# Two weight chunks of each layer by seven block products instead of eight, with sums of weight blocks made in DRAM

## The chip, the cores and the metric

One NeuronCore of one Trainium2 chip runs the kernel. The metric is the device time of one execution in microseconds (us). TensorE (PE) multiplies, VectorE (DVE) and ScalarE (ACT) do the elementwise work, GpSimd (POOL) does a little and issues some DMAs, and SyncE (SP) issues most of them. A loaded weight tile of TensorE ("PEld" in the profile) overlaps its matmuls.

## The reference

Two layers act on x, 256 tokens of 2048 channels. Each layer normalises, multiplies by `w_in` (seven kinds of columns), runs an mLSTM on eight heads and a gated linear recurrence (RG-LRU), gates both and adds their product with `w_out` to x.

```python
u = rms_norm(x, norm_g)
p = u @ w_in
qk, v, o, z_a, ig, fg, xb, z_b = jnp.split(p, SPLIT_AT, axis=-1)
...
h = mlstm_chunkwise(q, k, v, i_pre, log_f)
h = h * jax.nn.sigmoid(o.astype(f32)).reshape(b_, s_, H_A, DV_A)
...
y_a = h.astype(x.dtype) * jax.nn.silu(z_a)
xc = causal_dwconv(xb, lru_conv_w) + lru_conv_b
y_b = rg_lru(xc.astype(f32), w_a, b_a, w_x, b_x, lam).astype(x.dtype) * jax.nn.silu(z_b)
return x + jnp.concatenate([y_a, y_b], axis=-1) @ w_out
```

After both layers a last `rms_norm` gives the output. Everything is float32.

## The kernel before

**Chunks, units and halves.** Of each kind (qk, v, o, z, xb, zb) a layer has four groups g of 512 columns. A chunk, say z of group 2, is 256 tokens times 2048 inputs times 512 columns. Its weights come as four units of 1 MB (128 partitions of 2048 floats) from one DRAM array `ws`, and each unit is worked off in two halves. A half is 128 x 1024 floats, two blocks of 128 inputs by 512 columns.

**Three products for one.** A float32 product is made of three: ACT casts a half to a rounded part wH (L308), DVE subtracts to get the rest wL (L168, in the helper `tt_`), x is split alike into `x_s`, and TensorE multiplies high by high, high by low and low by high (L332). With two blocks of 128 inputs, two blocks of 128 tokens and three products, a half of a plain chunk is 12 matmuls of 128x512. A chunk is 8 halves, 96 matmuls. Its sums for both token blocks stay in two PSUM banks (`new_acc`), from which posts such as `o_post` and `z_post` read.

**Order.** `_sequence` lists the units: for each layer and group the chunks o, qk, v, the products with `w_out` of the group before (`out`), xb, z, the gate product (L761, from `xcs`, the split result of the convolution of xb) and zb. The main loop walks the halves. It splits weights three halves ahead of TensorE (AHEAD), into four buffers each of wH and wL, and loads ahead of that into three buffers of 1 MB (`raw`, L275 and L277, SP's queue). The other work of DVE and ACT (convolutions, softmax-like gates, scans) stands in generators in the list `bg`. After every half `pump` lets them go on for a budget, 1.05 with up to two generators in the list and 2.6 with more. `require` runs them until a named result is there. A scheduler then sets each engine's own order, so that work without a dependency can move far ahead.

**DRAM.** Results change from token to channel order through DRAM: SP writes `moved` (L449), POOL reads it back as `fr` (L450). The residual x stands in DRAM (`x_d`) and POOL adds the products of `out` to it by adding transfers (L901, `accum_op`), half a megabyte each.

**PSUM** has eight banks: two pairs for chunks and four banks for small products, in two tags `aux0` and `aux1` with two buffers each.

Of the kernel before, what the change touches and what calls it, by code (L numbers as in the profile page):

```python
# [63 lines left out]

def _plan():

    return list(dict.fromkeys(item for item, _ in _sequence()))
# [17 lines left out]
def tile_trunk(ctx, tc, x, xt, par, gw, gb, ws, final_g, out):  # L85
# [30 lines left out]
    def new_x_acc():  # L116
        st["xa"] = act.tile([P, 2, D], F32, tag="xacc", name="x_acc")

    def load_x_acc():
        new_x_acc()  # L120
        for c in range(4):
            nc.sync.dma_start(out=st["xa"][:, :, 512 * c : 512 * c + 512], in_=xd[c])

    def store_x(c):
        S.dma_start(out=xd[c], in_=st["xa"][:, :, 512 * c : 512 * c + 512])
# [14 lines left out]

    def load_x(c):
        if c == 0:
            nc.sync.dma_start(out=pars[:, 0, 16:NPAR], in_=par[:, 16:NPAR])
            nc.sync.dma_start(out=pars[:, 1, :], in_=par[:, NPAR : 2 * NPAR])
            nc.sync.dma_start(out=gbs, in_=gb.rearrange("h (l c) -> h l c", l=DEPTH))
            for l in range(DEPTH):
                nc.sync.dma_start(out=gwr[l], in_=gw[l])
            new_ss()
        cs = slice(512 * c, 512 * c + 512)
        nc.sync.dma_start(out=st["xa"][:, :, cs], in_=xv[:, :, cs])  # L150
# [7 lines left out]
    gwr = [small.tile([P, KT, 16], F32, tag="gwr", name=f"gwr{l}") for l in range(DEPTH)]  # L158
# [44 lines left out]
    def tl_lam(nm):  # L203
        return small.tile([P, DEPTH, 16], F32, tag=f"lam_{nm}", name=f"lam_{nm}", bufs=1)

    def lam_gen():
        ql = log1p_exp_half(lam, tl_lam, st["split_end"])
# [11 lines left out]
    bg = deque()  # L219
    timed = []  # L220

    def pump(budget):
        st["credit"] = min(st["credit"] + budget, budget)
        i = 0
        while i < len(bg) and st["credit"] > 0:
            try:
                c = next(bg[i])
            except StopIteration:
                del bg[i]
                continue  # L230
            if c is None:
                break
            if c == "wait":
                i += 1
            else:
                st["credit"] -= c

# [21 lines left out]
    def load_unit(hf):  # L259
        n = st["nload"]  # L260
        st["nload"] += 1
        item, j = hf["at"]
        raw = hf["box"]["raw"] = wraw.tile([P, 2048], F32, tag="raw", name="raw")
        if n < 4:
            w = 512 if n == 0 else 1024
            u = blocks[item, j]
            for o in range(0, 2048, w):
                if o % 1024 == 0:
                    load_xt(n, o // 1024)
                nc.sync.dma_start(out=raw[:, o : o + w], in_=ws[u][:, o : o + w])  # L270
        elif hf["paired"]:
# [14 lines left out]
    def prepare(hf):  # L286
# [16 lines left out]
        opening = n < 4  # L303
# [74 lines left out]
    def rms_stats(l):  # L378
# [6 lines left out]
        st["rstd", l] = rstd  # L385

# [22 lines left out]
    def square_sum(c):  # L409
        for t in range(2):  # L410
            junk = work.tile([P, 512], F32, tag="sF", name="junk")
            S.activation(out=junk, in_=st["xa"][:, t, 512 * c : 512 * c + 512], func=AF.Square,
                         accum_out=st["ss"][:, t, c : c + 1])
# [148 lines left out]
    def e_gen(l, g):  # L562
        while ("nG", l) not in st:
            yield "wait"
        nb = small.tile([P, 2, T], F32, tag="nb", name="nb", bufs=1)
# [26 lines left out]
    def o_post(l, g, acc):  # L592
# [4 lines left out]
        rstd = st["rstd", l]  # L597
# [18 lines left out]
    def qk_post(l, g, acc):  # L616
# [3 lines left out]
        def gen():  # L620
# [18 lines left out]
            while ("E", l, g) not in st or ("v", l, g) not in st:  # L639
                yield "wait"  # L640
            E, em, so, (vH, vL) = st["E", l, g], st["em", l], st["so", l, g], st["v", l, g]
            Pt = work.tile([P, 2, 384], F32, tag="Pt", name="Pt")
# [243 lines left out]
    def out_chunk(l, g, c):  # L886
# [9 lines left out]
        def postfn():  # L896
# [9 lines left out]
            x_acc = st["xa"]  # L906
# [6 lines left out]
            xs = x_acc[:, :, cs]  # L913
            if c == 3:
                tt_(xs, xs, ps, ALU.add)
            for t in range(2):
                xt_ = x_acc[:, t, cs].rearrange("p (c m j) -> p c m j", c=4, m=4)
# [22 lines left out]

    def layer_start(l):
# [7 lines left out]
    def emit_in(l, kind, g):  # L949
        def first_gen(acc):  # L950
            gates(l)
# [12 lines left out]
            yield from gates_tr(l)  # L964

# [8 lines left out]
    def last_out(l, g):  # L974
# [11 lines left out]
        def acc(c, t):  # L986
            if (c, t) not in accs:
# [3 lines left out]
                else:  # L991
                    accs[c, t] = aux("acc_x")
# [16 lines left out]
        def add(c, t, ps, at=0):  # L1009
            xs = st["xa"][:, t, 512 * c + at : 512 * c + at + ps.shape[-1]]  # L1010
# [23 lines left out]
        def finish(t):  # L1034
# [5 lines left out]
            for c in (2, 0, 3, 1):  # L1040
                cs = slice(512 * c, 512 * c + 512)
                xs = st["xa"][:, t, cs]
# [50 lines left out]
    for item in dict.fromkeys(i for i, _ in seq):  # L1093
        kind, l, g = item[0], item[1], item[-1]
        halves = []
# [10 lines left out]
    order_ = [dict(hf, at=(item, j)) for item, j in seq for hf in units[item][j]]  # L1106

    nprep = 0
    for n, hf in enumerate(order_):
# [14 lines left out]
        pump(1.05 if len(bg) <= 2 else 2.6)  # L1124
# [95 lines left out]
```

## Time and profile before

| | |
|---|---|
| time, median of 3 runs | 1491.46 us (1490.43 to 1492.03) |
| the profiled execution | 1491.23 us |
| its span, first to last instruction | 1489.5 us |
| granted TensorE clock | 0.998 |
| ACT busy, DVE busy | 931.6 us (63%), 1060.1 us (71%) |
| moved by DMA | 345.65 MB, mean 232 GB/s |

The profile is of one execution. A row of a group gives line, engine, operation, output and inputs, shape, count, then busy time and the mean duration of one, then the engine's idle time before these instructions and what ended it. A window row gives the busy time of each engine in a stretch, the granted clock, the busy share of the 16 DMA engines and what they moved.

### The profile page before, as it was taken

How to read it: one execution, taken by the hardware profiler on the slowest of the kernel's cores; microseconds unless marked ns; L12 is line 12 of the kernel's file. 1: busy time of each engine (PE TensorE's matmuls, PEld its weight loads, DVE VectorE, ACT ScalarE, POOL GpSimd, SP SyncE). 2: the span in 40 equal slices, each digit the busy share in tenths (PEclk: the TensorE clock that was granted, in tenths of full speed). 3: DMA queues.
4: the chain of work that ended last, by engine and by line, in shares of the span. 5: the costliest groups of instructions: out<-in, count | busy, mean ns of one | idle time of the engine just before them, and what ended most of it. 6: DMA issues, size and time to landing. Idle time of an engine off the chain costs nothing.

```text
span 1489.5 us, 18487 instructions
## 1 busy us (share of the span) xinstructions
PE 1479.5 (99%) x6830; PEld 1236.0 (83%) x6830; DVE 1060.1 (71%) x1448; ACT 931.6 (63%) x1199; POOL 83.1 (6%) x154
## 2 busy tenths in 40 slices
PE   9999999999999999999999999999999999999997
PEld 7888888888888888888888888888888888888886
DVE  6788866676568855778867788765855778557785
ACT  7756864575565845658575667645755567555675
POOL 0020100000000000000000101000000000000002
PEclk9999999999999999999999999999999999999999
DMA  9866767866677666886785766578667777578783
GB/s 341 294 221 223 232 211 214 254 225 214 202 238 234 217 225 216 253 264 226 264 280 193 242 215 240 205 206 250 225 223 214 239 225 234 200 227 269 231 283 109
DMA packets 91370, 345.65 MB, mean 232 GB/s; under 512 B 9984, under 2 KB 30480, under 8 KB 69776
## 3 DMA queue, kind: packets, MB, share of 16 engines
q1 hardware_dynamic: 79472, 306.44, 60.5%
q0 software_dynamic: 9344, 33.58, 9.3%
q10 hardware_dynamic: 2464, 4.47, 0.8%
q8 instruction: 53, 0.87, 0.2%
q14 instruction: 37, 0.30, 0.1%
HBM read 307.20 MB, written 37.24 MB: 231 GB/s over the span
## 4 chain that ended last, share of the span: by engine, by line
PE 96%; DVE 2%; DMA 1%; ACT 1%; issue 0%; POOL 0%; SPq 0%; DVEq 0%; ACTq 0%; POOLq 0%
PE acc L332 86%; PE ps_gt L761 3%; PE acc L345 2%; DVE wL L168 1%; DMA fr<-moved 1%; PE acc L1004 1%; PE acc L1003 1%; PE acc L1002 1%; PE ps_g L499 0%; PE acc_x L1004 0%; PE acc_x L1003 0%; PE acc_x L1002 0%; PE ps_S L648 0%; PE ps_n L590 0%; PE ps_n L588 0%
## 5 line engine op out<-in xcount | busy, mean ns | idle before, releaser
L332 PE MATMUL acc<-wH,x_s 128*128 128x512 f32 x3008 | 930.1, 389 | 0.0
L168 DVE TENSOR_TENSOR wL<-raw,wH 128x1024 fp32r<-128x1024 f32 (+1 forms) x532 | 636.9, 1205 | 326.4 <-ACT wH L308 325.7
L308 ACT CAST wH<-raw 128x1024 fp32r<-128x1024 f32 (+1 forms) x532 | 547.5, 1036 | 393.0 <-PE acc L332 364.7
L332 PEld LDWEIGHTS acc<-wH,x_s 128*128 128x128 f32 x3008 | 564.6, 188 | 117.0
L332 PE MATMUL acc<-wL,x_s 128*128 128x512 f32 x1504 | 584.1, 389 | 0.4 <-DVE wL L168 0.4
L332 PEld LDWEIGHTS acc<-wL,x_s 128*128 128x128 f32 x1504 | 282.3, 188 | 59.1 <-DVE wL L168 0.8
L332 PE MATMUL acc<-wH,yaH 128*128 128x512 f32 x224 | 87.6, 391 | 0.0
L332 PE MATMUL acc<-wH,ybL 128*128 128x512 f32 x224 | 87.3, 390 | 0.0
L332 PE MATMUL acc<-wH,ybH 128*128 128x512 f32 x224 | 87.2, 389 | 0.0
L332 PE MATMUL acc<-wL,ybH 128*128 128x512 f32 x224 | 87.2, 389 | 0.0
L332 PE MATMUL acc<-wH,yaL 128*128 128x512 f32 x224 | 87.2, 389 | 0.0
L332 PE MATMUL acc<-wL,yaH 128*128 128x512 f32 x224 | 87.2, 389 | 0.0
L446 DVE STREAM_TRANSPOSE blk<-tok 128x1024 f32<-128x1024 f32 x33 | 40.9, 1238 | 18.5 <-ACT tok L436 18.5
L436 ACT ACTIVATE tok<-acc,rstd 128x512 f32<-128x512 f32 x46 | 29.1, 685 | 32.9 <-PE acc L332 32.9
L332 PEld LDWEIGHTS acc<-wH,ybL 128*128 128x128 f32 x224 | 42.0, 188 | 9.1 <-DVE ybL L168 0.3
L332 PEld LDWEIGHTS acc<-wH,yaL 128*128 128x128 f32 x224 | 42.0, 188 | 8.9
L332 PEld LDWEIGHTS acc<-wH,ybH 128*128 128x128 f32 x224 | 42.0, 188 | 8.5
L332 PEld LDWEIGHTS acc<-wL,ybH 128*128 128x128 f32 x224 | 42.0, 188 | 8.5
L332 PEld LDWEIGHTS acc<-wL,yaH 128*128 128x128 f32 x224 | 42.1, 188 | 8.3
L332 PEld LDWEIGHTS acc<-wH,yaH 128*128 128x128 f32 x224 | 42.1, 188 | 8.3
L171 DVE SCALAR_TENSOR_TENSOR xc<-ch,pars,xc 128x255 f32<-128x255 f32 (+2 forms) x96 | 43.0, 475 | 4.4 <-ACT xc L420 4.4
L450 POOL DMA_DIRECT2D fr<-moved x34 | 18.8, 554 | 479.4 <-DMA moved<-blk 260.3
(208 smaller groups left out, 1282.1 us busy)
## 6 DMA issues: line engine op xcount, KB each, us to landing
raw<-in_ws_dram SPq DMA_DIRECT2D x168, 1024.0 KB, 5.3
raw<-in_ws_dram SPq DMA_DIRECT2D x190, 512.0 KB, 4.9
fr<-moved POOLq DMA_DIRECT2D x34, 512.0 KB, 5.8
moved<-blk SPq DMA_DIRECT2D x132, 128.0 KB, 2.4
x_d<-stage POOLq DMA_DIRECT2D x24, 512.0 KB, 5.4
x_d<-x_acc ACTq DMA_DIRECT2D x8, 512.0 KB, 7.4
x_acc<-x_d SPq DMA_DIRECT2D x8, 512.0 KB, 4.3
xp<-in_xt_dram SPq DMA_DIRECT2D x8, 256.0 KB, 6.9
```

The lines of the kernel that those rows point to most:

```text
L168: return V.tensor_tensor(out=o, in0=a, in1=b, op=op)
L171: return V.scalar_tensor_tensor(out=o, in0=a, scalar=s, in1=b, op0=op0, op1=op1)
L308: st["wH"] = S.copy(out=H[:, o], in_=r[:, o])
L332: st["mm"] = PE.matmul(o, a_[:, kt, P * t : P * t + P], W[:, k], start=b, stop=z)
L345: PE.matmul(ps[:, ct, T * part : 2 * T], W[:, k, P * ct : P * ct + P], moving, start=first and k == 0 and part == 0, stop=last and k == 3 ...
L436: S.activation(out=by_block(tok, t), in_=acc[:, t, :].rearrange("p (c m j) -> p c m j", c=4, m=4), func=AF.Copy, scale=rstd[:, t : t + 1])
L446: V.transpose(out=blk.rearrange("p m n -> p (m n)"), in_=tok.rearrange("p m c t j -> p (m c t j)"))
L450: back.dma_start(out=fr.rearrange("p a c t i -> p a (c t i)"), in_=moved)
L761: PE.matmul(o, W[:, ib, jl], xs[:, ib, a, :], start=j == 0 and i == 0 and W is Hv and a == 0, stop=i == 1 and W is Lv, skip_group_check=True)
L1002: PE.matmul(o, yH[:, kt, tsl], Hv[:, k, cs], start=start and k == 0, stop=False)
L1003: PE.matmul(o, yH[:, kt, tsl], Lv[:, k, cs], start=False, stop=False)
L1004: PE.matmul(o, yL[:, kt, tsl], Hv[:, k, cs], start=False, stop=stop and k == 1)
```

## The change

z of group 2 and o of group 3 of each layer (`PAIR`) are taken together as one product of 256 tokens by 1024 columns, cut in two along tokens, inputs and columns. Block products of 128 tokens by 1024 inputs by 512 columns would be eight; the change makes seven, of sums and differences of blocks, and adds their results up to the four output blocks.

- Each block product is four halves of six matmuls (two blocks of 128 inputs, one of tokens, three products) in one PSUM bank, and ends with a copy or with additions into an SBUF tile `res`. Its two weight units are loaded as two pairs of halves. The 14 pairs are spread evenly over the layer, from the start of v of group 0 to the place where z of group 2 stood; the 16 halves of z and o there go.
- Four sums of blocks of x (`block_sums`) are made by DVE and ACT: per sum two pieces, each of two or four DVE operations of 128x512, one to add the parts, a cast and a difference.
- The sums of weight blocks for products 5, 6, 7 and 4 (`weight_sums`) are made in DRAM: SP copies 512 KB pieces from `ws` to `w_d`, POOL adds others to them by adding transfers. Per layer these are 8 copies and 16 additions; 8 of the additions need no product to have been read before.
- The small products get three banks, `bank` takes the fourth. `z_post` and `o_post` of the pair read `res`. Tiles are placed anew to make room (x's accumulator in two tiles that the sums share, `Pt` in `ch`, `nb` in `sD`, `gwr` in `c4`).

```diff
+PAIR = (("z", NG - 2), ("o", NG - 1))
...
     def aux(name):
-        st["aux"] = 1 - st["aux"]
-        return psum.tile([P, 512], F32, tag=f"aux{st['aux']}", name=name, bufs=2)
+        st["aux"] = (st["aux"] + 1) % 3
+        return psum.tile([P, 512], F32, tag=f"aux{st['aux']}", name=name)
+
+    def bank(name):
+        return psum.tile([P, 512], F32, tag="bank", name=name)
...
+        def made(i, key, terms):
+            to = sums[i]
+            for k in (0, 4):
+                ks = slice(k, k + 4)
+                two = [work.tile([P, 4, P], F32, tag=tag, name="sum_t") for tag in ("tok", "blk")]
+                for a in range(2):
+                    terms(two, a, k, ks)
+                tt_(two[0], two[0], two[1], ALU.add)
+                S.copy(out=to[:, 0, ks], in_=two[0])
+                tt_(to[:, 1, ks], two[0], to.bitcast(F32)[:, 0, ks], ALU.subtract)
+                yield 2.6
...
+        yield from made(0, "S1", s1)
+        yield from made(1, "S4", s4)
+        while ("done", l, 3) not in st:
+            yield "wait"
+        yield from made(1, "S2", s2)
+        yield from made(0, "S3", s3)
...
+        def moved(to, start, r, c):
+            for j in range(2):
+                for h in range(2):
+                    cs = slice(1024 * h, 1024 * h + 1024)
+                    src = block_unit(l, r, c, j)[:, cs]
+                    if start:
+                        nc.sync.dma_start(out=wd[l][to][j][:, cs], in_=src)
+                    else:
+                        G.dma_start(out=wd[l][to][j][:, cs], in_=src, accum_op=ALU.add)
...
+        yield from moved(0, True, 0, 0)
+        yield from moved(0, False, 0, 1)
+        yield from moved(1, True, 1, 1)
+        yield from moved(1, False, 0, 1)
+        while ("loaded", l, 5) not in st:
+            yield "wait"
+        yield from moved(0, False, 1, 1)
...
+                for k in range(2):
+                    aH, aL = A(2 * kp + k)
+                    PE.matmul(box["b"], aH, Hv[:, k], start=kp == 0 and k == 0, stop=False)
+                    PE.matmul(box["b"], aH, Lv[:, k], start=False, stop=False)
+                    PE.matmul(box["b"], aL, Hv[:, k], start=False, stop=kp == 3 and k == 1)
...
+            (1, plain(0, 0), None, lambda: copied(1), (0, 0)),
+            (2, plain(0, 1), None, lambda: add(0, 1, box["b"]), (1, 0)),
+            (5, summed(0), "S1", lambda: copied(3), 0),
+            (3, summed(1), "S4", lambda: add(2, 3, box["b"]), (1, 1)),
+            (6, summed(1), "S2", end6, 0),
+            (7, summed(0), "S3", end7, 1),
+            (4, plain(1, 1), None, end4, 0),
...
+            at = a + (i + 1) * (b - a) // len(pairs)
...
-        pump(1.05 if len(bg) <= 2 else 2.6)
+        pump(1.05 if sum(g not in aside for g in bg) <= 2 else 2.6)
```

The order on three queues shows where this lands. First **SP's queue early in layer 0** (`raw` are weight loads, `moved` the detour through DRAM; of `w_d`, the first digit is the layer). Before:

```order
L275 DMA raw_749<-in_ws_dram 128x1024 x2
L275 DMA raw_802<-in_ws_dram 128x1024 x2
L275 DMA raw_838<-in_ws_dram 128x1024 x2
L275 DMA raw_885<-in_ws_dram 128x1024 x2
L275 DMA raw_928<-in_ws_dram 128x1024 x2
L449 DMA moved_971<-blk_968 32x4x256 x4
```

The same stretch of SP's queue now:

```order
L303 DMA raw_756<-in_ws_dram 128x1024 x2
L1026 DMA w_d001_119<-in_ws_dram 128x1024
L1026 DMA w_d010_120<-in_ws_dram 128x1024 x2
L296 DMA raw_819<-in_ws_dram 128x2048
L1026 DMA w_d011_121<-in_ws_dram 128x1024
L303 DMA raw_861<-in_ws_dram 128x1024 x2
L1026 DMA w_d011_121<-in_ws_dram 128x1024
L1026 DMA w_d100_122<-in_ws_dram 128x1024
L303 DMA raw_906<-in_ws_dram 128x1024 x2
L303 DMA raw_941<-in_ws_dram 128x1024 x2
L1026 DMA w_d100_122<-in_ws_dram 128x1024
L303 DMA raw_997<-in_ws_dram 128x1024 x2
```

Seven copies now stand among five weight loads, and those of layer 1 (`w_d100`) are among them: the scheduler moved them up beside layer 0's. All 16 copies of both layers stand between the eleventh and the thirty-second weight unit of 276.

Second, **POOL's queue in the same stretch**. Before:

```order
L450 DMA fr_591<-moved_593 128x1024
L539 DMA nG_d0_117<-scs_545 8x256
L567 DMA nb_720<-nG_d0_117 128x512
L557 COPY at0_739<-scs_545 32x16 x4
L557 COPY at1_740<-scs_545 32x16 x4
L567 DMA nb_1665<-nG_d0_117 128x512
L582 AFFINE_SELECT E_768<-E_768 128x128 x4
L450 DMA fr_969<-moved_971 128x1024
```

Now (L1028 are the adding transfers):

```order
L1028 DMA w_d001_119<-in_ws_dram 128x1024
L1028 DMA w_d010_120<-in_ws_dram 128x1024 x2
L613 AFFINE_SELECT E_776<-E_776 128x128 x4
L1028 DMA w_d011_121<-in_ws_dram 128x1024 x2
L1028 DMA w_d100_122<-in_ws_dram 128x1024 x2
L481 DMA fr_989<-moved_991 128x1024
```

Seven additions stand ahead of this `fr`, and 16 of both layers' additions stand in this early part.

Third, **DVE's queue in the same stretch**, where the mLSTM's gates (`scs`) end. Before:

```order
L168 TENSOR_TENSOR wL<-raw,wH 128x1024
L171 SCALAR_TENSOR_TENSOR scs<-scs 8x256
L175 TENSOR_SCALAR scs<-scs 8x256
L541 STREAM_TRANSPOSE scs<-scs 64x256
L168 TENSOR_TENSOR wL<-raw,wH 128x1024
L171 SCALAR_TENSOR_TENSOR qc<-ch,pars,qc 128x254
L171 SCALAR_TENSOR_TENSOR qc<-ch,pars,qc 128x255
L171 SCALAR_TENSOR_TENSOR qc<-ch,pars,qc 128x253
```

Now, from shortly behind that place on:

```order
L186 TENSOR_TENSOR sum_t<-x_s 128x512 x2
L186 TENSOR_TENSOR wL<-raw,wH 128x1024
L186 TENSOR_TENSOR sum_t<-sum_t 128x512
L186 TENSOR_TENSOR wL<-raw,wH 128x1024
L186 TENSOR_TENSOR sums_786<-sum_t,sums_786 128x512
L186 TENSOR_TENSOR sum_t<-sums_786,x_s 128x512 x2
L186 TENSOR_TENSOR sum_t<-sum_t,x_s 128x512 x2
L186 TENSOR_TENSOR wL<-raw,wH 128x1024
L186 TENSOR_TENSOR sum_t<-sum_t 128x512
L186 TENSOR_TENSOR wL<-raw,wH 128x1024
L186 TENSOR_TENSOR sums_787<-sum_t,sums_787 128x512
L186 TENSOR_TENSOR wL<-raw,wH 128x1024
```

The sums of x's blocks stand between the splits of the weights that TensorE is about to use, 20 such operations in the first part of each layer.

More of the change, by code (lines that the diff above doesn't have):

```diff
@@ L157, in tile_trunk @@
     gbs = const.tile([NH, DEPTH, 2], F32, name="gbs")
-    gwr = [small.tile([P, KT, 16], F32, tag="gwr", name=f"gwr{l}") for l in range(DEPTH)]
+    gwr = []
     ident = const.tile([P, P], F32, name="ident")
@@ L270, in load_unit @@
                 nc.sync.dma_start(out=raw[:, o : o + w], in_=ws[u][:, o : o + w])
+        elif item is None:
+            nc.sync.dma_start(out=raw, in_=hf["from"])
+            if "loaded" in hf:
+                st[hf["loaded"]] = True
         elif hf["paired"]:
@@ L590, in mm3, with o_post @@
         PE.matmul(o, aL, bH, start=False, stop=last)
-    def o_post(l, g, acc):
+    def o_post(l, g, acc, sign="rstd"):
         if g > 0:
@@ new lines, in block_unit, with weight_sums @@
+    def block_unit(l, r, c, j):
+        return ws[blocks[("in", l) + PAIR[c], 2 * r + j]]
+    wd = [[[dram.tile([P, 2048], F32, name=f"w_d{l}{i}{j}") for j in range(2)] for i in range(2)] for l in range(DEPTH)]
+    def weight_sums(l):
+        def moved(to, start, r, c):
[8 more added lines that the diff above has]
+                    yield "wait"
+                    yield "wait"
+        yield from moved(0, True, 0, 0)
[3 more added lines that the diff above has]
+        while ("loaded", l, 5) not in st:
+            yield "wait"
+        yield from moved(0, False, 1, 1)
+        while ("loaded", l, 6) not in st:
+            yield "wait"
+        yield from moved(0, False, 1, 0)
```

149 lines of the change are left out of this document (126 added, 23 removed).

## Prediction

> **What bounds the kernel now.** I read the page's busy times and chain first, then TensorE's waits, then the longest pieces of the chain of waits.
>
> ```profile
> PE 1479.5 (99%) x6830; PEld 1236.0 (83%) x6830; DVE 1060.1 (71%) x1448; ACT 931.6 (63%) x1199; POOL 83.1 (6%) x154
> PE 96%; DVE 2%; DMA 1%; ACT 1%; issue 0%; POOL 0%; SPq 0%; DVEq 0%; ACTq 0%; POOLq 0%
> PE ps_blank L110 <- DVE blank L108: 1.3, 1, 1.3
> PE acc L332 <- DVE wL L168: 0.4, 1, 0.4
> 312.42 130.58 PE acc L332 x576
> ```
>
> TensorE waits 1.7 us in all, so time can only be won by giving it less to do, and everything else matters only where it makes TensorE wait. The last row prices a matmul: 576 of 128x512 took 130.58 us, 0.2267 us each (the group rows' 389 ns is one matmul's length, and they overlap).
>
> A second look is at how near the others are to being late. These are two windows over the start of each layer's stretch in which the change adds work, and the chain of waits around 200 us.
>
> ```profile
> core 0: us, PE busy (x) PEld busy (x) DVE busy (x) ACT busy (x) POOL busy (x), PEclk, DMA share, GB/s
> 46.00:153.00 107.00, 107.00 (x509) 89.99 (x508) 91.47 (x159) 69.38 (x90) 10.23 (x21) 1.00 0.71 233
> 794.00:889.00 95.00, 95.00 (x456) 80.00 (x455) 80.39 (x146) 59.20 (x76) 8.90 (x21) 1.00 0.68 218
> ...
> 183.34 9.05 DMA fr<-moved
> ...
> 201.52 1.15 DVE wL L168
> 202.67 0.04 issue
> 202.71 13.71 PE acc L332 x59
> ```
>
> DVE is busy 85% of both windows, and the DMA engines about 70%. Near 200 us the chain runs through DMA `fr` and DVE, and TensorE goes on 0.04 us after the split that it needs: there it has no slack at all, though it loses nothing yet.
>
> **The change part by part.** *TensorE.* Per layer 8 block products (192 matmuls, two chunks of 96) become 7 of 24, 168. That is 24 fewer in each of two layers: 48 x 0.2267 = **10.9 us** off the span. It holds only if everything below hides.
>
> *Weight splits.* 28 halves per layer take the place of 16, so 24 more in all, and a block half gives TensorE six matmuls, 1.36 us, for the same cast and subtraction.
>
> ```profile
> L168 DVE TENSOR_TENSOR wL<-raw,wH 128x1024 fp32r<-128x1024 f32 x516 | 625.9, 1221 | 323.7 <-ACT wH L308 323.1
> L308 ACT CAST wH<-raw 128x1024 fp32r<-128x1024 f32 x516 | 537.6, 1049 | 389.9 <-PE acc L332 364.7 <-DMA raw<-in_ws_dram 9.6 <-ACT wH L308 4.0
> 102.30 3.45 DVE L168 TENSOR_TENSOR wL<-raw,wH 128x1024 fp32r<-128x1024 f32 x3
> L168 DVE TENSOR_TENSOR tok<-hh,za 128x512 f32<-128x512 f32 x16 | 11.1, 693 | 0.6
> ```
>
> Back to back a split costs DVE 3.45 / 3 = 1.15 us, so 24 cost 28 us; ACT's casts cost 24 x 1.05 = 25 us. A pair of block halves takes DVE 2.3 us of the 2.7 us that TensorE spends on it. Spread over two stretches of some 400 us this alone hides.
>
> *Sums of x blocks and of results.* Per layer 36 operations of 128x512 for the sums and 8 for `res`, at 0.69 us (the `tok` row has that shape; 0.62 back to back as far as the split's 1221 against 1150 shows). 88 x 0.65 = 57 us in both layers. DVE goes from 1060 to 1060 + 28 + 57 = 1145 of 1479 us, 77%: no bound on average. In the windows it is. S1 and S4 put 20 operations (13 us) there, and three pairs put 6 splits (6.9 us) there and give TensorE 3 x 12 x 0.2267 = 8.2 us. Window one: 91.5 + 19.9 = 111.4 us of work in 107 + 8.2 = 115.2 us; window two: 100.3 in 103.2. DVE would be 97% busy for 100 us, in an order that is fixed, and it has waits of its own that no backlog fills:
>
> ```profile
> 91.28 1.01 DVE L176 TENSOR_SCALAR E<-nb,at 128x256 f32<-128x256 f32 x4 [2.16 <-DMA nb<-nG_d]
> 96.51 1.23 DVE L168 TENSOR_TENSOR qc<-qc,qsg 128x1024 f32<-128x1024 f32 x1 [1.15 <-ACT qsg L630]
> 116.59 0.48 DVE L171 SCALAR_TENSOR_TENSOR xc<-ch,pars,xc 128x255 f32<-128x255 f32 x1 [1.23 <-ACT xc L420]
> ```
>
> These are 4.5 us in window one, with 3.8 us left. Each layer can therefore lose 0 to 6 us; I take 3 for layer 1, and 1 for layer 0 beside the next term, during which DVE catches up. What is late then is the split of the next half, behind the convolution or the sum that stands ahead of it.
>
> *DMA in layer 0.* All 16 copies and 16 of the additions of both layers stand early in layer 0 (the order of SP's and POOL's queues above), so in window one, with three more units of 0.5 MB than its matmuls would need. The trace has no copy from DRAM to DRAM and no addition from DRAM. The nearest rows are weight loads mixed with stores at full rate, and the addition of `stage` to `x_d`, which was issued at 229.84 us:
>
> ```profile
> q1 hardware_dynamic: 79472, 306.44, 60.5%
> raw<-in_ws_dram SPq DMA_DIRECT2D x168, 1024.0 KB, 5.3
> x_d<-stage POOLq DMA_DIRECT2D x24, 512.0 KB, 5.4
> 30.00:40.00 10.00, 10.00 (x46) 8.03 (x45) 4.54 (x5) 6.51 (x13) 0.00 (x0) 1.00 1.04 410
> 230.00:236.00 6.00, 6.00 (x33) 5.14 (x32) 4.52 (x14) 2.48 (x3) 0.75 (x1) 1.00 0.94 209
> ```
>
> A piece is 0.524 MB. Lower end: at 410 GB/s a copy holds the engines 1.28 us; an addition at the rate of the second window, 209 GB/s, 2.5 us. Then window one needs 107 x 233 / 410 = 61 us for what it moves now, plus 16 x 1.28 + 16 x 2.5 = 60, plus 4 for the block units, 125 of 115 us. Upper end: by busy share. Window one uses 0.71 x 107 = 76 us; a copy costs 0.524 x 2.94 = 1.5 us (901 us of queue q1 for 306.44 MB), an addition 3.5 us (0.94 x 6 = 5.6 us, less 2.1 for the 0.73 MB of loads in that window at 2.94). That is 76 + 24 + 56 + 5 = 161 of 115 us, 46 late. What a stream can be late: a load of 5.3 us is issued four units of 5.44 us ahead of the matmuls (three buffers, splits three halves ahead) and its first split takes 2.3, so 21.8 - 5.3 - 2.3 = 14 us. **TensorE waits between 0 (10 late, hidden by 14) and 32 us.** The additions need not be done by then, so not all lateness falls on the weights; that lowers the upper end to about 20. Between the ends I take 10: the additions are nearest to the `x_d` row, which has the dearer price.
>
> The Trainium skill, page "DMA: Bandwidth & Descriptors", section "Issuing engines are not separate DMA queues", says that transfers of SP, ACT and POOL share the same 16 engines and interleave. This speaks against the change, and the trace agrees: with one addition under way the engines were 94% busy at 209 GB/s. The same page, section "Latency and other measured facts", gives 207 to 214 GB/s per direction for tile copies from HBM to HBM. By it a copy would take an estimated 2.5 us in place of 1.28, the lower end would be 30 us late in place of 10, TensorE's wait 16 us and the time 1502; no run here shows such a copy.
>
> *Gate of group 2.* Its matmuls need `xcs`, made from xb, and z's four units no longer stand between.
>
> ```profile
> 443.04 1.26 ACT L436 ACTIVATE tok<-acc,rstd 128x512 f32<-128x512 f32 x2 [1.67 <-PE acc L332]
> L168 DVE TENSOR_TENSOR xcs<-xc,xcs x2: 673/680/687, 468.8 to 474.6; 128x512 fp32r<-128x512 f32 x2
> 444.11 10.97 PE acc L332 x48
> ```
>
> From xb's end to the last `xcs` went 475.3 - 443.0 = 32.3 us. What is left for TensorE in between is four `out` units, 2 x 10.97 = 21.9 us, 24 small matmuls of 0.12, and a block pair of 2.7, 27.5 us, and some 2 us of zb that the scheduler put ahead. `require` now hurries the convolution. The wait is 0 to 3 us per layer; I take 1.
>
> *The rest* counts as nothing: three banks for small products instead of four (no wait for a bank is in the rows), the moved tiles, `res` read by `z_post`. The cover is TensorE's own matmuls; without it, each is below 0.5 us.
>
> Sum, from this execution's 1491.23 us (0.23 under the median; its span plus 1.73): -10.9 + 10 + 1 + 3 + 2 = +5.1, **1496 us**.
>
> **The rivals.**
>
> - *Everything hides* (faster). Copies run at the full rate beside loads, and DVE's own waits shrink as it falls behind. Then TensorE loses 0 to 6 us: 1491.2 - 10.9 + 0 to 6 = 1480 to 1486. For it: the first windows show 410 GB/s with loads and stores mixed, and 14 us of lead. Against it: 97% of DVE. It decides at a DMA lateness of 14 us in layer 0.
> - *The early DMA costs its upper end* (much slower): 20 us in layer 0, and 5 more in its second burst of six copies: 1491.2 - 10.9 + 25 + 6 = 1511, 1504 to 1517. For it: the busy share of the addition. Against: additions can run late unnoticed.
> - *The change doesn't do what it says*: TensorE wins 10.9 us but SP's queue, in order, stands at a load of `w_d` until the last addition has landed, and the loads behind it with it. The additions for products 6 and 4 start only after a product has loaded. There are about 29 us between pairs, against 5.4 us for an addition, so it is unlikely; a wait over 14 us would cost some 3 us at 4 places, 1492.
>
> **How the numbers follow.** My forecast, a late weight stream and a full DVE, has 0.42 (1488 to 1504); all hidden 0.34; the dear DMA 0.17; the stalled queue 0.07. The range from 1481 to 1512 leaves out about the ends of the second and the third. A measurement of this kernel can tell about 0.2%, 3 us, from no change. Faster than 1488.5: 0.34 and a little of the first, 0.37; within 3 us: 0.17; slower: 0.46.
>
> **What would show it.** In the new profile: 48 fewer matmuls of 128x512; waits of TensorE on `wL` between 75 and 160 us, with ACT's casts waiting for `raw` there (DMA) or not (DVE); busy DMA near 1.0 from 75 to 150 us; landing of `raw` well over 5.3 us there; DVE over 95% in both windows; a wait at `ps_gt` at the gate of group 2. I am wrong if the DMA share stays below 0.9 there, or if ACT never waits for `raw`.

## The result, and the profile after

| | before | after |
|---|---|---|
| median, four runs each | 1491.12 us | 1538.42 us (1537.56 to 1541.39) |
| the profiled execution, its span | 1491.23, 1489.5 us | 1541.39, 1539.7 us |
| granted TensorE clock | 0.998 | 0.986 |

The change makes the kernel slower: 1.032 times, 95% interval 1.0302 to 1.0338, 47.3 us. The forecast was 1496, its range ended at 1512.

The page of the changed kernel, with the busy times, the granted clock in 40 slices, the two DMA queues that carry nearly all (q0 is GpSimd's; packets, MB, share of 16 engines) and the chain's shares:

```profile
PE 1490.2 (97%) x6782; PEld 1232.9 (80%) x6782; DVE 1138.8 (74%) x1562; ACT 964.4 (63%) x1242; POOL 112.5 (7%) x186
PEclk9999889999999999999999999999999999999999
q1 hardware_dynamic: 83504, 327.41, 60.8%
q0 software_dynamic: 13952, 50.35, 15.6%
PE 74%; DMA 10%; DVE 5%; issue 5%; ACT 5%; SPq 1%; POOL 0%; ACTq 0%; POOLq 0%; DVEq 0%
```

TensorE has its 48 matmuls fewer (6782 for 6830), yet its busy time has grown by 10.7 us and its idle time from 10.0 to 49.5. So of the 50.2 us that the span is longer, 39.5 are idle time and 10.7 are busy time. Since 10.9 us of matmuls came off, those that are left were busy for 21.6 us more. The chain, 96% TensorE before, now runs 10% of the span through DMA. What TensorE and ScalarE waited for (total, times, longest):

```profile
PE acc L360 <- DVE wL L186: 17.2, 14, 5.7
PE acc L360 <- ACT wH L336: 13.2, 7, 9.1
PE ps_gt L792 <- ACT gate L797: 5.4, 1, 5.4
...
ACT wH L336 <- DMA raw<-in_ws_dram: 72.9, 32, 8.3
```

ScalarE's casts waited 9.6 us for `raw` before and 72.9 now. Windows show where and how:

```profile
core 0: us, PE busy (x) PEld busy (x) DVE busy (x) ACT busy (x) POOL busy (x), PEclk, DMA share, GB/s
46.00:153.00 107.00, 93.08 (x385) 73.90 (x385) 81.66 (x138) 54.71 (x69) 26.80 (x28) 0.95 0.98 291
834.00:929.00 95.00, 93.83 (x423) 76.76 (x422) 84.25 (x136) 55.13 (x69) 6.90 (x19) 1.00 0.65 216
75.00:225.00 150.00, 119.80 (x505) 96.02 (x504) 106.61 (x164) 82.01 (x109) 29.69 (x33) 0.89 0.91 273
96.00:102.00 6.00, 0.30 (x2) 0.25 (x2) 3.65 (x8) 1.78 (x2) 3.07 (x3) 0.88 1.03 137
102.00:108.00 6.00, 6.00 (x16) 4.70 (x17) 6.00 (x9) 2.62 (x3) 6.00 (x1) 0.55 1.00 124
176.00:183.00 7.00, 1.04 (x6) 0.52 (x4) 4.79 (x9) 6.68 (x9) 0.81 (x1) 0.72 1.02 383
183.00:190.00 7.00, 6.78 (x23) 5.93 (x24) 5.32 (x6) 6.35 (x14) 0.81 (x1) 0.55 0.94 188
207.00:216.00 9.00, 0.60 (x3) 0.17 (x1) 0.00 (x0) 2.03 (x5) 0.00 (x0) 0.65 0.54 203
216.00:224.00 8.00, 6.87 (x16) 5.08 (x17) 7.36 (x7) 5.96 (x8) 0.00 (x0) 0.54 0.20 59
125.00:127.00 2.00, 2.00 (x5) 1.61 (x6) 2.00 (x2) 0.00 (x0) 0.00 (x0) 0.50 1.02 274
184.00:189.00 5.00, 5.00 (x19) 4.32 (x18) 4.32 (x5) 4.35 (x8) 0.81 (x1) 0.50 0.86 143
```

From 75 to 225 us TensorE is idle for 30.2 of 150 us, with the DMA engines 91% busy; layer 1's stretch (second row) loses 1.2. Then read the fourth to the ninth row in pairs: TensorE hardly works in the first of a pair (0.30, 1.04 and 0.60 us busy; the waits are 5.7, 5.4 and 9.1 us long), and the granted clock of the stretch behind is 0.55, 0.55 and 0.54. These are means, since the clock comes back before the stretch ends: from 184 to 189 us it is 0.50 (last row). A shorter wait did the same: TensorE stood for 2.55 us from 122 us on, and from 125 to 127 us the clock is 0.50. The third row's 0.89 over 150 us is part of the 21.6 us.

What TensorE stood for is in the chain of waits (start, length):

```profile
86.38 5.88 DMA nG_d<-scs
92.55 5.71 DMA nb<-nG_d
...
99.36 1.20 DVE sum_t L186 x2
...
111.49 16.41 DMA raw<-in_ws_dram
...
164.34 11.82 DMA raw<-in_ws_dram
188.70 11.57 DMA moved<-blk
200.90 13.05 DMA fr<-moved
...
215.67 0.94 ACT wH L336
```

Not only the weights `raw` are late, but small detours through DRAM too: `nG_d` ahead of the first wait, `moved` and `fr` ahead of the longest. Operations that wait for them, and at the first wait a sum of x blocks as well (`sum_t`), stand ahead of the next split of weights. `fr` was issued 0.6 us after `moved` had landed (200.27 us), so there the time went by between issue and landing, not in GpSimd's queue. The issues of 75 to 225 us (count, KB, median us to landing):

```profile
raw<-in_ws_dram SPq DMA_DIRECT2D x11, 1024.0 KB, 8.9
raw<-in_ws_dram SPq DMA_DIRECT2D x18, 512.0 KB, 11.3
w_d<-in_ws_dram SPq DMA_DIRECT2D x13, 512.0 KB, 9.6
w_d<-in_ws_dram POOLq DMA_DIRECT2D x13, 512.0 KB, 10.5
moved<-blk SPq DMA_DIRECT2D x12, 128.0 KB, 8.2
fr<-moved POOLq DMA_DIRECT2D x3, 512.0 KB, 9.4
nG_d<-scs POOLq DMA_DIRECT2D x1, 8.0 KB, 5.9
```

The same stretch of run e2 below, which has none of these copies and additions:

```profile
raw<-in_ws_dram SPq DMA_DIRECT2D x18, 512.0 KB, 4.8
moved<-blk SPq DMA_DIRECT2D x16, 128.0 KB, 3.1
fr<-moved POOLq DMA_DIRECT2D x4, 512.0 KB, 5.1
nG_d<-scs POOLq DMA_DIRECT2D x1, 8.0 KB, 1.6
```

`nb` is not among the late ones at the first wait: its 5.71 us compare with a median of 5.3 in the kernel before.

### The profile page after: what moved, and what is told of

It reads as the page before. It is cut to its first block, busy times and chain, and to the rows that moved or that the text cites. A ratio compares the mean times of both kernels' runs of the same rounds, so it can differ in the third digit from the quotient of the medians.

```text
span 1539.7 us, 18745 instructions
## 1 busy us (share of the span) xinstructions
PE 1490.2 (97%) x6782; PEld 1232.9 (80%) x6782; DVE 1138.8 (74%) x1562; ACT 964.4 (63%) x1242; POOL 112.5 (7%) x186
## 2 busy tenths in 40 slices
DMA packets 100014, 383.44 MB, mean 249 GB/s; under 512 B 10944, under 2 KB 31440, under 8 KB 76880
## 3 DMA queue, kind: packets, MB, share of 16 engines
q0 software_dynamic: 13952, 50.35, 15.6%
## 4 chain that ended last, share of the span: by engine, by line
PE 74%; DMA 10%; DVE 5%; issue 5%; ACT 5%; SPq 1%; POOL 0%; ACTq 0%; POOLq 0%; DVEq 0%
PE acc L360 62%; DMA raw<-in_ws_dram 6%; DVE wL L186 2%; PE ps_gt L792 2%; ACT wH L336 2%; DMA moved<-blk 2%; PE acc L373 1%; DMA fr<-moved 1%; PE ps_b L1092 1%; PE ps_b L1093 1%; PE ps_b L1091 1%; DMA nb<-nG_d 1%; DVE xc L189 1%; DMA nG_d<-scs 1%; PE acc L1187 1%
## 5 line engine op out<-in xcount | busy, mean ns | idle before, releaser
L360 PE MATMUL acc<-wH,x_s 128*128 128x512 f32 x2752 | 862.0, 392 | 13.3 <-ACT wH L336 13.2
L186 DVE TENSOR_TENSOR wL<-raw,wH 128x1024 fp32r<-128x1024 f32 (+1 forms) x556 | 663.4, 1202 | 284.5 <-ACT wH L336 282.6
L336 ACT CAST wH<-raw 128x1024 fp32r<-128x1024 f32 (+1 forms) x556 | 570.2, 1037 | 390.7 <-PE acc L360 277.7
L360 PEld LDWEIGHTS acc<-wH,x_s 128*128 128x128 f32 x2752 | 520.7, 189 | 124.5 <-ACT wH L336 16.7
L360 PE MATMUL acc<-wL,x_s 128*128 128x512 f32 x1376 | 540.3, 394 | 17.3 <-DVE wL L186 17.2
L360 PEld LDWEIGHTS acc<-wL,x_s 128*128 128x128 f32 x1376 | 260.6, 189 | 78.1 <-DVE wL L186 24.4
L792 PE MATMUL ps_gt<-xcs,wH 128*128 128x256 f32 x256 | 47.3, 284 | 5.4 <-ACT gate L797 5.4
L792 PEld LDWEIGHTS ps_gt<-xcs,wH 128*128 128x128 f32 x256 | 41.1, 192 | 6.5 <-ACT gate L797 5.7
```

The source lines that it names most:

```text
L186: return V.tensor_tensor(out=o, in0=a, in1=b, op=op)
L336: st["wH"] = S.copy(out=H[:, o], in_=r[:, o])
L360: st["mm"] = PE.matmul(o, a_[:, kt, P * t : P * t + P], W[:, k], start=b, stop=z)
L792: PE.matmul(o, W[:, ib, jl], xs[:, ib, a, :], start=j == 0 and i == 0 and W is Hv and a == 0, stop=i == 1 and W is Lv, skip_group_check=True)
```

## The experiments

The theory at the start was that the transfers of the weight sums, of both layers at once, fill the DMA engines early in layer 0. The rivals were a full VectorE and GpSimd's queue, in which additions wait for copies ahead of `fr`. Times are medians; the ratio is to the kernel before on the same chip, with its 95% interval.

### Parts taken out

**e1** keeps layer 1's copies out of layer 0:

```diff
-                        nc.sync.dma_start(out=wd[l][to][j][:, cs], in_=src)
+                        i0 = nc.sync.dma_start(out=wd[l][to][j][:, cs], in_=src)
+                        if l > 0:
+                            order(i0, st["mm"])
```

> The copies of layer 1's weight sums are held to where the program writes them, behind a matmul of layer 1, so they and their additions no longer stand in layer 0; nothing else moves. Theory (transfers: the weight sums of both layers together fill the DMA engines from 75 to 225 us, raw, moved and fr land late, TensorE idles and its granted clock falls): of the 58 us between 1538.4 and the 1480 of the case where everything hides, more than half comes back, 1490 to 1512 us, the granted clock in 100 to 225 us is back near 1.00, and layer 1 loses 0 to 8 us. Rival (VectorE is full because of the sums of x blocks): nothing comes back, 1532 to 1540. Rival (GpSimd's queue: additions stand ahead of fr and wait there for their copies, whatever the load): layer 0's own additions still stand ahead of fr, so less than half comes back, 1512 to 1530, and layer 1 now loses like layer 0.

**e2** has no transfers for sums:

```diff
-            beside(weight_sums(l))
...
-                src = block_unit(l, *W, j) if isinstance(W, tuple) else wd[l][W][j]
+                src = block_unit(l, *(W if isinstance(W, tuple) else (0, 1)), j)
```

> No copies and no additions: the four products that use a sum of weight blocks load a plain block instead, of the same size, so the output is another. Everything else stays. Theory (transfers): all of it comes back, 1480 to 1487 us. Rival (VectorE full): 1525 to 1540. Rival (GpSimd's queue): like the theory, 1480 to 1487, so this run parts only VectorE from the two others.

**e3** has no sums of x blocks, and no product waits for one:

```diff
-            beside(block_sums(l))
...
-            return lambda kt: tuple(st["sums", l][i][:, a, kt] for a in range(2))
+            return plain(0, i)
...
```

> The sums of x blocks are left out (32 additions and subtractions of VectorE and 8 copies of ScalarE per layer; the products take plain x blocks, so the output is another); all copies and additions of weights stay. Theory (transfers): little changes, 1528 to 1540 us. Rival (VectorE full): 1480 to 1495. Both at once in equal parts: 1505 to 1520.

**e4** is both edits.

> Neither the transfers of the weight sums nor the sums of x blocks; the seven products and the additions into res are left. All theories: the 48 fewer matmuls show alone, 1491 - 10.9 = 1480 to 1482 us. If it is above 1486, block pairs that need a 1 MB load and two splits for 2.7 us of TensorE cost something by themselves, which no theory here has.

| run | us | ratio |
|---|---|---|
| e1 | 1517.40 | 1.0174 (1.0159 to 1.0189) |
| e2 | 1503.32 | 1.0081 (1.0064 to 1.0098) |
| e3 | 1544.02 | 1.0348 (1.0332 to 1.0363) |
| e4 | 1494.87 | 1.0024 (1.0015 to 1.0033) |

The transfers cost 1538.4 - 1503.3 = 35.1 us, and 21.0 of them come back when layer 1's copies, and the additions behind them, leave layer 0. The sums of x blocks on VectorE as the main cause are out: without them the time is 5.6 us longer, not shorter. With the transfers gone the same sums cost 1503.3 - 1494.9 = 8.4 us. The costs don't simply add up: without the sums the transfers cost 1544.0 - 1494.9 = 49.1 us.

e1 and e2 are slower than the theory of the transfers said (1490 to 1512, 1480 to 1487). e1's time lies in the range of GpSimd's queue, but the rest of that forecast isn't there: beside e2, TensorE works 7.9 us less from 75 to 225 us (138.10 and 145.97) and only 2.9 less from 800 to 960 us (153.29 and 156.20), so layer 1 doesn't lose like layer 0. In e1 `nG_d` still lands after 6.1 us, and the wait behind it is 6.6 us: layer 0's own transfers are enough for that.

What no theory had: with neither, the kernel is still slower than before, 14.7 us above 1491.1 - 10.9. That became the second question.

### Copies and additions apart

**e6** leaves the additions out (the line `G.dma_start` becomes `pass`), **e7** makes them plain copies to DRAM that nothing reads, **e8** additions to such DRAM:

```diff
-                        G.dma_start(out=wd[l][to][j][:, cs], in_=src, accum_op=ALU.add)
+                        G.dma_start(out=dram.tile([P, 1024], F32, name="aside"), in_=src, accum_op=ALU.add)
```

> The 16 copies stay where they are, the 32 additions are left out (the sums are then single blocks, so the output is another). With neither the time was 1503.3, with both 1538.4. Theory (additions are the dear part: twice as many, each reads two pieces and writes one): 1505 to 1513. Rival (the copies are the dear part, six of them from 0.5 MB each in a burst): 1522 to 1535.

> The 32 additions become plain copies of the same piece, on the same queue at the same places, into DRAM that nothing reads: same bytes read from the weights and written, but no second read, and no wait of GpSimd's queue for a copy to land (so the output is another). Theory (the engines are full of bytes): 1520 to 1538. Rival (GpSimd's queue stands waiting for the copies, and fr, nG_d and nb behind it): 1503 to 1512. If the price is in the addition itself (its second read): 1508 to 1520, and the next run says so.

> As the run before, but as additions, onto DRAM that no copy fills: the additions' whole traffic, and no wait for a copy. Theory (traffic): 1530 to 1540, near the changed kernel's 1538. Rival (the queue's waits): 1503 to 1512, as the run before. If additions are dearer than copies by their second read, this run stands 8 us or more above the run before.

e6 took 1506.13 us (1.0102, 1.0087 to 1.0117), e7 1548.87 (1.0387, 1.0371 to 1.0402), e8 1584.83 (1.0627, 1.0611 to 1.0643). The 16 copies cost some 2.8 us over e2, so the additions cost the other 32.3. e7 and e8 miss their numbers for a reason of their own: with nothing to wait for, the pieces went out from the program's start, on top of its first loads. GpSimd's timeline in e8:

```profile
3.21 6.97 POOL L1028 DMA_DIRECT2D aside<-in_ws_dram  x8
```

So they don't tell the queue's waits from traffic over the whole run; what they show is that the additions cost more, not less, where no wait holds them back. They do price a piece: q0 takes 14.0% of 1583.9 us in e8 and 11.7% of 1547.4 in e7, against 9.0% of 1504.5 in e6. That is 86 and 46 us for 32 pieces, **2.7 us of all 16 engines for an addition and 1.4 for a copy**.

### Why the seven products alone give nothing back

In e4 TensorE's waits for a split are these:

```profile
PE acc L360 <- DVE wL L186: 5.9, 8, 1.1
PE acc L360 <- ACT wH L336: 1.4, 4, 0.4
```

They are only a part of the 14.7 us. In the profiled execution of e4 TensorE is idle for 16.9 us, 6.9 more than before, and busy for 1476.3, 7.7 more than 1479.5 - 10.9. A matmul's record lasts 0.389 us while the next starts 0.227 us later, so a delay below 0.16 us counts as busy time. The longer waits lie beside the gates and the convolution of group 2, such as here, on VectorE (start, us, line, operation):

```profile
503.67 1.66 DVE L189 SCALAR_TENSOR_TENSOR xc<-ch,pars,xc 128x253 f32<-128x253 f32 x4
505.24 1.23 DVE L186 TENSOR_TENSOR wL<-raw,wH 128x1024 fp32r<-128x1024 f32 x1
506.39 2.57 DVE L189 SCALAR_TENSOR_TENSOR xc<-ch,pars,xc 128x253 f32<-128x253 f32 x6
508.91 2.36 DVE L186 TENSOR_TENSOR wL<-raw,wH 128x1024 fp32r<-128x1024 f32 x2
```

Ten operations of the convolution and a split stand between 503.7 and 508.9 us, while TensorE works off a block pair in 2.7. Five edits of e4 follow. **e5** puts a full half between the two halves of a pair (and finds the next load in the order that this makes); **e9** moves the pair behind the gate of group 0 by eight halves and the next by four; **e10** puts zb before the gate of group 2:

```diff
-            order_[at:at] = pairs[i]
+            one, two = pairs[i]
+            order_[at:at] = [one]
+            order_[at + 2 : at + 2] = [two]
...
-            at += at % 2
+            at += at % 2 + {2: 8, 3: 4}.get(i, 0)
...
-            items.insert(len(items) if g > 0 else -2, ("in", l, "zb", g))
+            items.insert({0: -2, 2: -1}.get(g, len(items)), ("in", l, "zb", g))
```

> As e4 (no transfers of weight sums, no sums of x blocks), but the two halves of a block pair no longer stand side by side: one half of the next full unit is put between them, so each split that TensorE waits for has at least one full half (2.7 us) of lead beside the block halves (1.36 us each). e4 stood at 1494.9 where 1480 was expected, with 14.9 us of stalls behind block pairs near the gates. Theory (the lead is counted in halves, three of them, and a block half is worth half as much time): most of the 14.9 us come back, 1481 to 1487 us. Rival (VectorE or ScalarE has too much to do near the gates, in whatever order): 1491 to 1496.

> As e4 (neither transfers of weight sums nor sums of x blocks, 1494.9 us), but the block pair that stands right behind the gate of group 0 is moved 8 halves on, and the next one 4; nothing else. In e4 TensorE stalled 2.8 us between 150 and 175 us and some 2 us at the same place of layer 1, at that pair. Theory (a block pair beside a gate asks for two casts and two subtractions in 2.7 us while ScalarE and VectorE do the gate's work): these stalls go, 1489 to 1492 us. Rival (the gate's work costs the same stall wherever the pairs stand, since the weight splits are too many on the whole): 1494 to 1496.

> As e4, but zb's four units of group 2 stand before that group's gate and not behind it, so that TensorE again has 21.8 us of work where z's four units stood in the kernel before. In e4 it stalled 3.0 us from 500 to 600 us and 3.4 us from 1200 to 1300 us, around the gate of group 2, behind the convolution on VectorE and the gate's chain. Theory (the hole that z left ahead of the gate): most of these 6 us come back, 1488 to 1491 us. Rival (the pair before the gate, or the number of splits): 1493 to 1497.

**e13** leaves out the subtraction of the block halves; **e14** the cast too (its matmuls read x in place of weights, so they don't wait for the loads either):

```diff
+            L = H if "from" in hf else wsp.tile([P, 2, 512], F32R, tag="L", name="wL")
...
+            if "from" not in hf:
+                st["wL"] = tt_(L[:, o], r[:, o], H.bitcast(F32)[:, o], ALU.subtract)
```

> As e4 (seven products, no sums of weights or of x blocks; 1494.9 us), but the 56 block halves leave out their subtraction on VectorE, 1.15 us each, and multiply by the cast half twice; loads, casts and matmuls stay. Theory (VectorE has no room for the 28 splits per layer that take the place of 16, between the gate's and the convolution's operations): 1483 to 1488 us. Rival (ScalarE's casts): 1490 to 1495. Rival (neither, the pairs' loads or the order of the program): 1493 to 1497.

> As the run before, but the block halves leave out the cast as well: their matmuls take x as the moving side and wait for no weight, while the weights are still loaded. Theory (the splits): all stalls of e4 above those of the kernel before go, 1480 to 1484 us. Rival (the hole ahead of the gate of group 2, which these matmuls don't fill): 1486 to 1489. Rival (loads or order): 1493 to 1497.

| run, beside e4's 1494.87 | us | ratio to the kernel before |
|---|---|---|
| e5 | 1499.01 | 1.0050 (1.0033 to 1.0067) |
| e9 | 1498.96 | 1.0051 (1.0036 to 1.0066) |
| e10 | 1492.14 | 1.0010 (1.0001 to 1.0020) |
| e13 | 1489.29 | 0.9991 (0.9981 to 1.0000) |
| e14 | 1487.30 | 0.9973 (0.9964 to 0.9982) |

Two ideas fell: spreading the halves and moving the pair each made it 4.1 us worse. The hole that z left is worth some 2.7 us, not much beyond the two intervals. The subtractions are worth 5.6 us, and the casts, or the loads that they wait for, 2.0 more, so the splits account for about 7.6 of the 14.7. In e14 TensorE's waits for a split are down to this:

```profile
PE acc L363 <- DVE wL L186: 1.6, 2, 0.9
```

The 7.1 us left, 1487.3 over 1480.2, are not settled. By its time e14 falls to the rival of the hole ahead of group 2's gate (1486 to 1489), but TensorE's waits in e14 have no `ps_gt`, and none for data is over 0.9 us. In its profiled execution (1486.0 us) 1.4 us of the rest are idle time and 4.3 are busy time (1472.9 us), which fits many short delays; their cause these runs don't show.

### When the transfers cost

**e11** holds each piece behind the matmul at which it is written, one every four halves, layer 1's in the middle of layer 0; **e12** adds the edits of e9 and e10.

```diff
+                    order(i0, st["mm"])
+                    for _ in range(rest):
+                        yield "wait"
...
+            yield from weight_sums(1)
```

> The whole change with its output, but each copy and addition of weights is held behind the matmul at which it is written, one every four halves (11 us): layer 0's from about 85 us on, behind the transfers nG_d and nb of group 0, layer 1's behind them in the middle of layer 0. Same bytes, same number of transfers. Theory (it is the burst of both layers' transfers from 50 to 200 us that costs, not their number): of the 35 us that the transfers cost, 28 or more come back, 1503 to 1510 us. Rival (each addition costs wherever it runs, about 1 us each): 1525 to 1540.

> The paced transfers, the pair moved off the gate of group 0 and zb before the gate of group 2, together; the whole change with its output. If all three theories hold and their gains add: 1503 - 4 - 6 = 1493 to 1500 us, about the time of the kernel before or a little slower, since the sums of x blocks stay (8 us by the difference of two runs above). Rivals as in the three runs before.

e11 took 1542.11 us (1.0341, 1.0317 to 1.0364), e12 1537.37 (1.0307, 1.0291 to 1.0322). A clear miss: nothing came back. The loss had only moved, as e11's window from 225 to 500 us shows (in the changed kernel TensorE was busy 273.91 us there):

```profile
225.00:500.00 275.00, 260.92 (x1159) 215.07 (x1158) 181.48 (x220) 150.57 (x179) 26.23 (x37) 0.98 0.90 271
```

The pieces weren't paced, either. GpSimd works off its queue in order here: four additions gathered behind an addition into `x_d` that waited for 14.16 us. Its timeline, and from the chain of waits a load issued 9 us later:

```profile
320.93 0.88 POOL L932 DMA_DIRECT2D x_d<-stage  x1 [14.16 <-ACT stage L931]
321.47 3.70 POOL L1051 DMA_DIRECT2D w_d<-in_ws_dram  x4
```

```profile
330.95 19.87 DMA raw<-in_ws_dram
```

Four additions in a row, and a weight load beside them takes 19.9 us. They stand side by side; that the row is what held the load is not shown by this alone. Was it the additions as such? **e16** and **e17** put 16 additions alone into the kernel before, one every 24 or 6 halves:

```diff
+        if n >= 72 and n % 24 == 0 and st.setdefault("asides", 0) < 16:
+            st["asides"] += 1
+            order(G.dma_start(out=dram.tile([P, 1024], F32, name="aside"), in_=ws[st["asides"]][:, 0:1024], accum_op=ALU.add), st["mm"])
```

> The kernel before with 16 additions of 0.5 MB from the weights into DRAM that nothing reads, one every 24 halves (65 us) from about 205 us on; nothing else changes, the output neither. Theory (crowding: an addition holds the DMA engines some 3 us, which the spare quarter of the engines takes in when it comes alone): 1491 to 1495 us. Rival (each addition costs TensorE about 1 us wherever it runs): 1505 to 1512.

> The same 16 additions, one every 6 halves (16 us), from about 205 to 450 us. By crowding: 3 us in each 16 us is 19% on top of a share of 0.73 to 0.76, 0.92 to 0.95 of the engines, so some of it shows: 1495 to 1505 us. Rival (each costs 1 us wherever it runs): 1505 to 1512, the same as the run before.

e16 took 1491.68 us (1.0003, 0.9994 to 1.0012), e17 1490.96 (0.9999, 0.9989 to 1.0008). They cost nothing, where 1495 to 1505 had been expected of e17. In e17 several went out in twos and four even in a row, at 344.5 us, in the stretch where the DMA engines were least loaded. Windows of e17, columns as above:

```profile
200.00:300.00 100.00, 99.10 (x447) 81.85 (x446) 69.21 (x103) 54.94 (x63) 9.86 (x13) 1.00 0.84 247
300.00:400.00 100.00, 100.00 (x466) 83.76 (x465) 64.01 (x61) 60.00 (x74) 5.51 (x8) 1.00 0.77 252
400.00:500.00 100.00, 100.00 (x477) 84.20 (x476) 71.37 (x111) 64.16 (x80) 9.17 (x15) 1.00 0.84 252
```

**e18** is the whole change with each addition put behind another transfer of GpSimd's queue, or behind a matmul when seven halves have brought none. Layer 1's copies and its first eight additions run from 510 to 680 us, the other eight later, behind the loads that they wait for; **e19** adds the edit of e10:

```diff
+            k = next((i for i, t in enumerate(todo) if t[5] in st), None)
+            fresh = st.get("np", 0) > seen
+            if k is None or not (fresh or st["n"] - at >= LATE):
+                yield "wait"
+                continue
...
+            order(i0, st["pl"] if fresh else st["mm"])
```

> The whole change with its output; each addition is put right behind another transfer of GpSimd's queue (fr or the addition into x_d), one behind each, with one row of four left at the end of layer 0's; the copies go one every four halves in layer 0; layer 1's copies and additions run from about 510 to 800 us. Theory (rows of additions, which hold the loads behind them for 10 to 20 us, are the price, and a single one is hidden): near the run without transfers, 1503 to 1512 us, and no load of 1 MB above some 12 us outside the row of four. Rival (the amount: each piece costs about 0.7 us wherever it runs): 1530 to 1542.

> The same with zb before the gate of group 2, worth 2.7 us where nothing else was in the way: 1500 to 1510 us by the first theory, and still slower than the kernel before, since the sums of x blocks (8 us) and the splits of the block halves (8 us) stay.

e18 took **1507.00 us** (1.0114, 1.0097 to 1.0131): 31.4 of the 35.1 us are back with the same 383.44 MB, and the granted clock of the profiled execution is 0.999 (0.986 in the changed kernel). The longest load took 13.6 us, 1.6 more than expected. Its window from 75 to 225 us:

```profile
75.00:225.00 150.00, 144.06 (x659) 117.65 (x658) 132.46 (x199) 102.08 (x133) 30.59 (x34) 1.00 0.88 279
```

The DMA engines are nearly as busy as in the changed kernel (0.88 to 0.91), and TensorE works 24.3 us more. e19 is a miss: 1511.45 us (1.0138, 1.0123 to 1.0153); zb before the gate, worth 2.7 us by itself, costs 4.5 here. From 500 to 800 us, where layer 1's copies run, TensorE works 292.61 us in e19 and 297.64 in e18; why is open.

At least two things differ between e11 and e18, the rows of additions and the place of layer 1's pieces, so their shares aren't told apart. That rows of additions hold the loads behind them is therefore likely, not shown. No version with the whole output beats the kernel before, and e4 says why: with all sums free, the seven products still lost.

## Why the prediction was wrong, point by point

It had the sign and the main mechanism right (transfers early in layer 0 make the weights late), and the size wrong by 42 us. Its sum against what the runs give, as differences of medians taken in one order (e4, e2, the changed kernel), so that they add up:

| term | taken | measured |
|---|---|---|
| 48 matmuls | -10.9 | -10.9 by their count |
| weight splits and the rest, gate of group 2 | 0 and 2 | 14.7 (e4) |
| sums of x blocks and `res` | 4 | 8.4 (e2 less e4; without `res`) |
| transfers | 10 | 35.1 (after less e2) |

- **Transfers.** The price was right: 2.5 to 3.5 us for an addition and 1.28 to 1.5 for a copy stood there, 2.7 and 1.4 were measured (in the changed kernel, (15.6% of 1539.7 less 9.0% of 1504.5) / 32 = 3.3). The upper end of the lateness, 32 us, would have been close to 35.1, but partly by luck: the 35.1 hold what the lower clock cost, which that end left out. The step that failed is "not all lateness falls on the weights; that lowers the upper end to about 20", and the choice of 10 below it. What didn't fall on the weights fell on `nG_d`, `moved` and `fr`, on which VectorE and ScalarE wait in order, with the splits behind them. The sum had no term for these detours, though the chain before ran through `fr` without slack; there, at 202.7 us, TensorE even lost the 0.4 us of the prediction's list of waits.
- **The clock.** No term either. Behind each of the three long waits the clock is 0.50 for some us, and the stretches cost 6.00 x 0.45 + 6.78 x 0.45 + 6.87 x 0.46 = 8.9 us. They came with the transfers: TensorE's longest wait in e2 is 2.3 us. The Trainium skill, page "TensorE: Matmul & The Clock Gate", section "HAM oscillation — how this bites in real kernels", has the rule that an idle gap of TensorE above some 3.4 us drops its clock. The trace agrees for the three long waits; it differs in that the wait of 2.55 us before 125 us dropped the clock too.
- **Weight splits.** "Spread over two stretches of some 400 us this alone hides" failed. An average over 400 us says nothing of the few places where VectorE has ten operations of the convolution, or ScalarE a gate, ahead of the split of a pair that lasts 2.7 us. e13 and e14 show about 7.6 us of it; the other 7.1 are open.
- **Sums of x blocks.** Right in place, half in size: 8.4 for 4, of which 2.0 lie in the first window (TensorE works 104.96 of 107 us there in e2, 107.00 in e4). VectorE over 95% busy in both windows was wrong: 81.66 of 107 us and 84.25 of 95, since it waited itself. Without transfers, in e2, it is busy 99.11 of 107 us in the first window, near the forecast.
- **Gate of group 2.** The wait at `ps_gt`, 5.4 us, came at the gate of group 0, behind a late `raw`. The hole before group 2's gate costs some 2.7 us by e10, near the 2 taken, though e19 shows that this gain isn't kept in the whole kernel.
- **Rivals.** "Everything hides" had 0.34 and is refuted by e4, without a transfer or a sum. "The early DMA costs its upper end" was nearest, and its 20 + 5 us for transfers were too few.
- **The copy price by the skill.** From the figure of the Trainium skill, page "DMA: Bandwidth & Descriptors", section "Latency and other measured facts", the prediction estimated 2.5 us per copy; e7's copies, among loads of weights, held the engines 1.4 us, so the trace doesn't agree.

## What to carry to other kernels

Price a transfer by what it delays, not by its bytes: 16 additions of 2.7 us spread over 280 us cost nothing beside a TensorE-bound kernel, and 32 cost 32 us where a scheduler let half of them gather early, among loads and small detours through DRAM. Look up in the new order where transfers without a dependency went, and tie each to something that paces it in its own queue. Before counting a saving of matmuls, take out all that the change adds and measure the bare core: here it was already a loss, about half of it because a shorter unit leaves the same split half the time.

## What the runs showed of the hardware that wasn't expected

- With additions in place of copies beside the first loads, the 16 DMA engines are fully busy at two thirds of the rate: from 12 to 62 us in e8 share 1.06 at 243 GB/s, from 11 to 46 us in e7 1.01 at 371 GB/s.
- The granted clock is 0.50 behind a wait of TensorE of 5 to 9 us and back at 1.00 some 5.5 to 7 us after work resumes, so each of the three long waits cost some 3 us more than itself (2.7, 3.1 and 3.2). The shortest waits that dropped it are 2.3 us: behind one the clock is 0.50 in e1 (926 to 928 us), behind one as long it stays 1.00 in e18 (914 to 917 us).
- Additions of one queue landed one after another: the four that e17 issued within 2 us at 344.5 us landed 10.6, 14.7, 18.4 and 21.9 us after their issues.
